# One weight tile per product pass gets its low half from an adding DMA instead of VectorE

## The chip, the cores and the metric

The kernel is one launch on one NeuronCore of a Trainium2 chip. The metric is the device time of that launch in microseconds. A profile of one execution gives the span from the first to the last instruction of the program and every engine's instructions inside it. The engines are TensorE (PE in the profile; its weight loads are PEld), VectorE (DVE), ScalarE (ACT), GpSimd (POOL) and SyncE (SP). DMAs are issued from the instruction queues of SP, ACT and POOL and carried by 16 DMA engines.

## The reference, cut to what matters

The program is one layer of a decoder trunk on 256 tokens of width 2048, all in float32. The change lies in the feed-forward part, which is the last two lines of the layer:

```python
h = rms_norm(x, norm2_gain[l]) * (1 + scale2) + shift2
x = x + gate2 * swiglu(h, w_ffn_in[l], w_ffn_out[l])

def swiglu(h, w_ffn_in, w_ffn_out):
    gate, up = jnp.split(h @ w_ffn_in, 2, axis=-1)
    return (jax.nn.silu(gate) * up) @ w_ffn_out
```

The weights are `w_ffn_in` (2048 x 11264) and `w_ffn_out` (5632 x 2048). Ahead of it come the modulation from `c`, the input projection, three kinds of token mixing and the output projection.

## The kernel before

**Precision by halves.** TensorE is fed in a rounded float32 format (`F32R`). To keep float32 accuracy, every operand is held as a high half (the value rounded to that format) and a low half (value minus high half). A product then takes three matmuls, in `mm3` (L163 to L166): high by high (L164), high of the activations by low of the weights (L165), low of the activations by high of the weights (L166). Activations are the stationary operand, weights the moving one.

**A weight tile.** Weights arrive from HBM in tiles called `raw` of 128 partitions x 2 blocks of 128 rows x 512 columns, 512 KB each, by a DMA on SP's queue. ScalarE makes the high half `whi` by a copy into the rounded format. VectorE makes the low half `wlo` by subtracting the high half from `raw`. `raw`, `whi` and `wlo` each have four buffers that are used in rotation, so a tile's halves can be written once the tile four places earlier has had its last matmul.

**Where the work around the change lies.** The first feed-forward product runs over 11 units of 512 gate columns and 512 up columns. Units 1 to 7 (`FAST`) and the second product go through `fast_products` (L1296), which takes the contraction in pairs of row blocks, in an order that is written out: `PAIRS` for a unit, `OUT_A` and `OUT_B` for the two passes of the second product (columns 0 to 1023 and 1024 to 2047). An entry `(p, 0)` is a plain pair: two weight tiles, one for the columns at `c0` and one for those at `c1`, and 24 matmuls: the 12 of the tile at `c0`, then the 12 of the tile at `c1`. An entry `(p, 1)` is a fast pair: seven products (21 matmuls) on sums of weight blocks, with four tile slots taken in the rotation (`r0`, half of `r1`, and the two sum tiles `ta` and `tb`).

The entries that the change meets are those with `p = 2` that are plain: the fourth entry of `PAIRS` (behind the fast pair 6 and ahead of the fast pair 7), the third entry of `OUT_A` (behind two plain pairs) and the fourth entry of `OUT_B` (behind the fast pair 8).

**What sets the order.** The weights of a pair are requested three pairs ahead (`LOOK = 3`, L35, L1322) under `prio()`, which moves the loads and their splits ahead of other work in each engine's instruction order. Each engine runs its own instructions in the order in which they stand, and waits on semaphores. `load_pair` (L1264) is the function that loads and splits a pair; its inner `split` (L1272) holds the cast (L1276) and the subtraction (L1277), `raw_at` (L1267) the load (L1269). POOL issues some small loads in the first microseconds (L241 to L244), does one cast (L605), and is idle from then on.

Of the kernel before, what the change touches and what calls it, by code (L numbers as in the profile page):

```python
# [10 lines left out]
F32 = mybir.dt.float32  # L11
F32R = mybir.dt.float32r
U8 = mybir.dt.uint8
AF = mybir.ActivationFunctionType
ALU = mybir.AluOpType
AX = mybir.AxisListType

P = 128
# [5 lines left out]
NB = 512  # L24
# [8 lines left out]
RATE_IN, RATE_MID, RATE_FFN = 0.8, 0.6, 0.65  # L33
RATE_OUT = 2.5
LOOK = 3  # L35
DEFER = 4
AHEAD = 4000
WARM = (22, 38, 13)
# [38 lines left out]
def trunk(ctx: ExitStack, tc: tile.TileContext, I, out):  # L77
    nc = tc.nc
# [10 lines left out]
    def nm(base):  # L89
        uid[0] += 1  # L90
        return f"{base}_{uid[0]}"

    def S(tag, shape, dtype=F32):
        return slot.tile(shape, dtype, tag=tag, name=nm(tag))
# [13 lines left out]
    @contextmanager  # L108
    def prio(offset=AHEAD):

        with tc.high_priority(offset=offset):
            start = tc.cur_priority
            yield
            n = tc.cur_priority - start
        tc.cur_priority += n

    state = {"rate": 0.0}
# [4 lines left out]
    def tick(n):  # L122
        state["due"] = state.get("due", 0.0) + n
        while state["due"] >= 1.0:
            state["due"] -= 1.0
            for work in (bg, after):
                if work and next(work[0], "end") == "end":
                    work.pop(0)
# [39 lines left out]
    def block(pss, act, src, k0, k1, c0, base=0, w=None, tiles=range(NT), go_on=False, more=False, seeded=False,  # L168
# [7 lines left out]
        for k in range(k0, k1):  # L176
            if (k - k0) % 2 == 0 and tiles[-1] == NT - 1:
                tick(state["rate"])
            if k - k0 == DEFER and later:
                with tc.issue_after(state["mm"].ins), prio():  # L180
# [895 lines left out]
    for j in range(2):  # L1076
        hi = S(gtag[0][j], [P, 4, T], F32R)
        lo = S(gtag[1][j], [P, 4, T], F32R)
        for t in range(NT):
            o = og[t].rearrange("p h d -> p (h d)")  # L1080
            ps = misc_bank([P, 4, P])
            for i in range(4):
                c = 4 * j + i
                nc.tensor.transpose(ps[:, i, :], o[:, c * P : (c + 1) * P], ident)
            for par in range(2):
                gcol = vec[:, ROW_GG + par : ROW_GG + par + 1]
                src = ps[:, par:4:2, :]
# [176 lines left out]
    def load_pair(src, p, c0, c1, fast, tags):  # L1264


        def raw_at(c):  # L1267
            raw = wp.tile([P, 2, NB], F32, tag="raw", name=nm("raw"))
            nc.sync.dma_start(raw, src[2 * p * P : (2 * p + 2) * P, c : c + NB].rearrange("(k p) c -> p k c", p=P))  # L1269
            return raw  # L1270

        def split(src):  # L1272
            n = src.shape[1]
            hi = wp.tile([P, 2, NB], F32R, tag="whi", name=nm("whi"), bufs=4)
            lo = wp.tile([P, 2, NB], F32R, tag="wlo", name=nm("wlo"), bufs=4)
            nc.scalar.copy(hi[:, :n, :], src)  # L1276
            state["split"] = nc.vector.tensor_tensor(lo[:, :n, :], src, hi[:, :n, :].bitcast(F32), op=ALU.subtract)  # L1277
            return [(hi[:, i, :], lo[:, i, :]) for i in range(n)]

        sub = lambda dst, x, y: nc.vector.tensor_tensor(dst, x, y, op=ALU.subtract)  # L1280
        with prio():
            if not fast:
                return [split(raw_at(c0)), split(raw_at(c1))]
            r0, r1 = raw_at(c0), raw_at(c1)
            b11, b21 = split(r0)
            ta, tb = (S(tag, [P, 2, NB]) for tag in tags)
            sub(ta[:, 0], r1[:, 0], r0[:, 0])
            sub(ta[:, 1], r1[:, 1], r1[:, 0])
            (b22,) = split(r1[:, 1:2])
            sub(tb[:, 0], r1[:, 1], ta[:, 0])  # L1290
            sub(tb[:, 1], r0[:, 1], tb[:, 0])
            t1, t3 = split(ta)
            t2, t4 = split(tb)
            return b11, b21, b22, t1, t3, t2, t4

    def fast_products(src, c0, c1, order, at, sums, own, other, tags, hooks={}, more=False):  # L1296
# [4 lines left out]
        def load(n):  # L1301
            while len(ws) < min(n, len(order)):
                ws.append(load_pair(src, order[len(ws)][0], c0, c1, order[len(ws)][1], tags))

        load(LOOK if hooks else len(order))
        o = [[own([P, NB]) for _ in range(NT)] for _ in range(2)]
# [11 lines left out]
        for n, (p, fast) in enumerate(order):  # L1318
            tick(2 * state["rate"])
            if n in hooks:  # L1320
                hooks[n]()
            load(n + LOOK)  # L1322
            w = ws[n]
# [44 lines left out]
    for i in range(NFF):  # L1368
# [26 lines left out]
        hi = S(ftags[2 * i], [P, 4, T], F32R)  # L1395
        lo = S(ftags[2 * i + 1], [P, 4, T], F32R)
# [61 lines left out]
    n, pss = 3, o[1]  # L1458
# [43 lines left out]
```

## Time and profile before

| | |
|---|---|
| time, median of 3 runs (lowest to highest) | 1597.94 us (1597.09 to 1598.45) |
| the profiled execution's own time | 1597.22 us |
| its span, first to last instruction | 1595.4 us |
| TensorE busy | 1582.0 us, 99% |
| VectorE busy | 1275.5 us, 80% |
| ScalarE busy | 837.6 us, 53% |
| GpSimd busy | 5.3 us |
| bytes moved by DMA | 395.97 MB |

The profiled execution's time is 1.8 us over its span and 0.7 us under the median. The units 1 to 7 run from 918 us to 1220 us of the span, the first pass of the second product (`OUT_A`) from 1353 us, its second pass (`OUT_B`) from 1475 us.

In the rows of the profile, a group of instructions is given by its line in the kernel, the engine, the operation and the names of the tiles it writes and reads, with the count, the busy time and the mean of one in ns. A row of the timeline begins with the start in us from the span's start and the duration in us; in square brackets stands how long the engine was idle before it, and what ended that. The duration of a DMA row on a queue is that of issuing it; "us to landing" is from the start of issue until its last byte has been reported.

### The profile page before, as it was taken

How to read it: one execution, taken by the hardware profiler on the slowest of the kernel's cores; microseconds unless marked ns; L12 is line 12 of the kernel's file. 1: busy time of each engine (PE TensorE's matmuls, PEld its weight loads, DVE VectorE, ACT ScalarE, POOL GpSimd, SP SyncE). 2: the span in 40 equal slices, each digit the busy share in tenths (PEclk: the TensorE clock that was granted, in tenths of full speed). 3: DMA queues.
4: the chain of work that ended last, by engine and by line, in shares of the span. 5: the costliest groups of instructions: out<-in, count | busy, mean ns of one | idle time of the engine just before them, and what ended most of it. 6: DMA issues, size and time to landing. Idle time of an engine off the chain costs nothing.

```text
span 1595.4 us, 20167 instructions
## 1 busy us (share of the span) xinstructions
PE 1582.0 (99%) x7272; PEld 1308.2 (82%) x7272; DVE 1275.5 (80%) x1523; ACT 837.6 (53%) x1184; POOL 5.3 (0%) x14
## 2 busy tenths in 40 slices
PE   8999999999999999999999999999999999999998
PEld 7878888888888888888887888888888888778887
DVE  6889995888878787878756688888887677988884
ACT  5654449775754434444446655555454443554552
POOL 1000000000000000000000000000000000000000
PEclk9999999999999999999999999999999999999999
DMA  9999997667778889989766466556657889667664
GB/s 339 365 326 320 332 302 245 214 189 257 247 258 280 297 301 314 311 289 310 228 192 210 149 196 195 192 184 193 205 183 226 281 302 314 203 196 225 212 204 140
DMA packets 194596, 395.97 MB, mean 248 GB/s; under 512 B 12914, under 2 KB 27928, under 8 KB 194496
## 3 DMA queue, kind: packets, MB, share of 16 engines
q1 hardware_dynamic: 194096, 394.60, 75.0%
q8 instruction: 57, 0.93, 0.2%
q14 instruction: 43, 0.35, 0.1%
q10 hardware_dynamic: 176, 0.07, 0.0%
q0 software_dynamic: 224, 0.01, 0.0%
HBM read 392.53 MB, written 2.10 MB: 247 GB/s over the span
## 4 chain that ended last, share of the span: by engine, by line
PE 85%; DMA 5%; DVE 5%; ACT 3%; issue 2%; SPq 0%; ACTq 0%; DVEq 0%
PE acc L166 21%; PE acc L165 21%; PE acc L164 20%; PE misc L164 6%; PE misc L166 6%; PE misc L165 6%; DVE wlo L159 1%; ACT whi L158 1%; DMA AR<-w_ada 1%; DVE ada L288 1%; DMA raw<-w_br_gla 1%; DMA raw<-w_ffn_out 1%; PE acc L434 1%; DMA raw<-w_in 1%; PE misc L800 1%
## 5 line engine op out<-in xcount | busy, mean ns | idle before, releaser
L158 ACT CAST whi<-raw 128x1024 fp32r<-128x1024 f32 x362 | 368.6, 1022 | 412.2 <-PE acc L166 264.9
L159 DVE TENSOR_TENSOR wlo<-raw,whi 128x1024 fp32r<-128x1024 f32 x362 | 425.6, 1183 | 186.0 <-ACT whi L158 184.4
L164 PE MATMUL acc<-whi,H 128*128 128x512 f32 x1308 | 511.9, 392 | 1.2 <-ACT H L446 0.8
L165 PE MATMUL acc<-wlo,H 128*128 128x512 f32 x1308 | 510.9, 391 | 0.8 <-DVE wlo L159 0.7
L166 PE MATMUL acc<-whi,H 128*128 128x512 f32 x1308 | 509.8, 390 | 0.4 <-DVE H L453 0.4
L166 PEld LDWEIGHTS acc<-whi,H 128*128 128x128 f32 x1308 | 245.3, 188 | 52.9 <-DVE H L453 1.6
L164 PEld LDWEIGHTS acc<-whi,H 128*128 128x128 f32 x1308 | 245.5, 188 | 52.3 <-ACT H L446 1.3
L165 PEld LDWEIGHTS acc<-wlo,H 128*128 128x128 f32 x1308 | 245.7, 188 | 51.3 <-DVE wlo L159 1.7
L1276 ACT CAST whi<-raw 128x1024 fp32r<-128x1024 f32 (+1 forms) x184 | 179.2, 992 | 134.5 <-PE acc L166 68.0
L1277 DVE TENSOR_TENSOR wlo<-raw,whi 128x1024 fp32r<-128x1024 f32 (+1 forms) x184 | 205.2, 1145 | 19.8 <-ACT whi L1276 18.8
L164 PE MATMUL misc<-whi,H 128*128 128x512 f32 x246 | 96.1, 391 | 0.0
L165 PE MATMUL misc<-wlo,H 128*128 128x512 f32 x246 | 95.8, 389 | 0.0
L166 PE MATMUL misc<-whi,H 128*128 128x512 f32 x246 | 95.8, 389 | 0.0
L164 PE MATMUL acc<-whi,A 128*128 128x512 f32 x222 | 87.1, 394 | 0.5 <-ACT whi L1276 0.4
L165 PE MATMUL acc<-wlo,A 128*128 128x512 f32 x222 | 86.7, 390 | 0.8 <-DVE wlo L159 0.8
L166 PE MATMUL acc<-whi,A 128*128 128x512 f32 x216 | 84.3, 390 | 0.0
L288 DVE SCALAR_TENSOR_TENSOR ada<-AR,csil,ada 128x1024 f32<-128x1024 f32 x59 | 74.8, 1278 | 3.6 <-DMA AR<-w_ada 3.6
L165 PEld LDWEIGHTS misc<-wlo,H 128*128 128x128 f32 x246 | 46.2, 188 | 9.7 <-DVE wlo L1277 0.2
L166 PEld LDWEIGHTS misc<-whi,H 128*128 128x128 f32 x246 | 46.2, 188 | 9.5
L164 PEld LDWEIGHTS misc<-whi,H 128*128 128x128 f32 x246 | 46.2, 188 | 9.5
L164 PEld LDWEIGHTS acc<-whi,A 128*128 128x128 f32 x222 | 41.7, 188 | 9.6 <-ACT whi L1276 1.1
L165 PEld LDWEIGHTS acc<-wlo,A 128*128 128x128 f32 x222 | 41.7, 188 | 9.6 <-DVE wlo L159 1.1
(428 smaller groups left out, 1927.6 us busy)
## 6 DMA issues: line engine op xcount, KB each, us to landing
raw<-w_in SPq DMA_DIRECT2D x205, 512.0 KB, 4.8
raw<-w_ffn_in SPq DMA_DIRECT2D x176, 512.0 KB, 4.2
raw<-w_ffn_out SPq DMA_DIRECT2D x88, 512.0 KB, 4.8
AR<-w_ada SPq DMA_DIRECT2D x79, 512.0 KB, 5.1
raw<-w_out SPq DMA_DIRECT2D x32, 512.0 KB, 4.8
KC<-w_ada SPq DMA_DIRECT2D x30, 512.0 KB, 6.2
OS<-w_ada SPq DMA_DIRECT2D x16, 512.0 KB, 6.9
KD<-w_ada SPq DMA_DIRECT2D x16, 512.0 KB, 5.8
```

The lines of the kernel that those rows point to most:

```text
L158: state["cast"] = nc.scalar.copy(hi[:, :n, :], raw[:, :n, :])
L159: state["split"] = nc.vector.tensor_tensor(lo[:, :n, :], raw[:, :n, :], hi[:, :n, :].bitcast(F32), op=ALU.subtract)
L164: nc.tensor.matmul(ps, lh, rh, start=start, stop=False, skip_group_check=seeded)
L165: nc.tensor.matmul(ps, lh, rl, start=False, stop=False, skip_group_check=seeded)
L166: state["mm"] = nc.tensor.matmul(ps, ll, rh, start=False, stop=stop, skip_group_check=seeded)
L288: nc.vector.scalar_tensor_tensor(acc, raw, c, acc, op0=ALU.mult, op1=ALU.add)
L434: state["warm"] = nc.tensor.matmul(ps, ones_r, wide, start=True, stop=True)
L800: nc.tensor.matmul(ps[:n, t * N_GLA + h, :].rearrange("p (s l) -> p s l", l=L), at(f, h, t)[:, :n], odd(at(f, h, t)), start=True, stop=True,)
L1276: nc.scalar.copy(hi[:, :n, :], src)
L1277: state["split"] = nc.vector.tensor_tensor(lo[:, :n, :], src, hi[:, :n, :].bitcast(F32), op=ALU.subtract)
```

## The change

In `split`, a tile for which the weights' address is passed in as `again` gets its low half in two steps: ScalarE writes minus the high half into `wlo`, and a DMA issued from POOL's queue reads the same weights from HBM a second time and adds them to what stands in `wlo`. VectorE's subtraction isn't issued for that tile. It is passed in for the tile at `c1` of every plain pair with `p` in `ADDED`, which is `(2,)`: seven tiles in the units and one in each pass of the second product, nine in all.

```diff
+ADDED = (2,)
...
+        def weights(c):
+            return src[2 * p * P : (2 * p + 2) * P, c : c + NB].rearrange("(k p) c -> p k c", p=P)
+
         def raw_at(c):
             raw = wp.tile([P, 2, NB], F32, tag="raw", name=nm("raw"))
-            nc.sync.dma_start(raw, src[2 * p * P : (2 * p + 2) * P, c : c + NB].rearrange("(k p) c -> p k c", p=P))
+            nc.sync.dma_start(raw, weights(c))
             return raw
 
-        def split(src):
+        def split(src, again=None):
...
             nc.scalar.copy(hi[:, :n, :], src)
-            state["split"] = nc.vector.tensor_tensor(lo[:, :n, :], src, hi[:, :n, :].bitcast(F32), op=ALU.subtract)
+            if again is None:
+                state["split"] = nc.vector.tensor_tensor(lo[:, :n, :], src, hi[:, :n, :].bitcast(F32), op=ALU.subtract)
+            else:
+
+                nc.scalar.activation(lo, hi.bitcast(F32), AF.Copy, scale=-1.0)
+                nc.gpsimd.dma_start(lo, again, accum_op=ALU.add)
             return [(hi[:, i, :], lo[:, i, :]) for i in range(n)]
...
             if not fast:
-                return [split(raw_at(c0)), split(raw_at(c1))]
+                return [split(raw_at(c0)), split(raw_at(c1), weights(c1) if p in ADDED else None)]
```

## The prediction

> **What bounds the kernel now.** I read the page first: busy time, then the chain of work that ended last.
>
> ```profile
> span 1595.4 us, 20167 instructions
> ...
> PE 1582.0 (99%) x7272; PEld 1308.2 (82%) x7272; DVE 1275.5 (80%) x1523; ACT 837.6 (53%) x1184; POOL 5.3 (0%) x14
> ...
> PE 85%; DMA 5%; DVE 5%; ACT 3%; issue 2%; SPq 0%; ACTq 0%; DVEq 0%
> ```
>
> TensorE is busy for all but 13.4 us of the span. So what another engine saves is worth nothing unless TensorE was waiting for it, and any new wait of TensorE is paid in full. Next I asked for the stretches in which the nine tiles lie: units 1 and 2, the beginning of the first output pass, the beginning of the second.
>
> ```profile
> core 0: us, PE busy (x) PEld busy (x) DVE busy (x) ACT busy (x) POOL busy (x), PEclk, DMA share, GB/s
> 918.10:961.20 43.10, 43.10 (x195) 35.75 (x195) 35.93 (x43) 22.36 (x25) 0.00 (x0) 1.00 0.61 196
> ...
> 1352.80:1375.00 22.20, 21.38 (x100) 17.45 (x99) 20.30 (x21) 9.44 (x11) 0.00 (x0) 1.00 0.87 292
> 1475.20:1510.00 34.80, 34.80 (x155) 28.84 (x154) 29.58 (x35) 18.13 (x19) 0.00 (x0) 1.00 0.69 217
> ```
>
> In a unit TensorE is busy for 43.10 of 43.10 us; VectorE, at 35.93 us, is close behind but nobody waits for it. Then I followed one of the tiles on each engine: pair 2 of unit 1, ScalarE, VectorE, TensorE.
>
> ```profile
> 931.53 3.05 ACT L1276 CAST whi<-raw 128x1024 fp32r<-128x1024 f32 x3 [0.30 <-PE misc L166]
> ...
> 933.13 4.09 DVE L1277 TENSOR_TENSOR wlo<-raw,whi 128x1024 fp32r<-128x1024 f32 x4
> ...
> 934.69 0.39 PE L164 MATMUL misc<-whi,H 128*128 128x512 f32 x1
> ...
> 937.41 0.39 PE L164 MATMUL misc<-whi,H 128*128 128x512 f32 x1
> 937.63 0.39 PE L165 MATMUL misc<-wlo,H 128*128 128x512 f32 x1
> ```
>
> The three casts are the tile at c0, the tile at c1 (ours) and the first of fast pair 7. Each takes a third of 3.05 us, so ours ends near 933.55. It can't start much earlier: the first cast was released by TensorE's matmul, that is by a buffer of the rotation. VectorE's four subtractions run one after the other; ours is the second and ends near 935.5. TensorE begins the plain pair at 934.69, needs our high half at 937.41 and our low half at 937.63. So today the low half is about 2.1 us early, and it comes 4.1 us before its use at the very best, since the high half ends there.
>
> **The change part by part.**
>
> *VectorE's subtraction goes, nine times.*
>
> ```profile
> L1276 ACT CAST whi<-raw 128x1024 fp32r<-128x1024 f32 (+1 forms) x184 | 179.2, 992 | 134.5 <-PE acc L166 68.0
> L1277 DVE TENSOR_TENSOR wlo<-raw,whi 128x1024 fp32r<-128x1024 f32 (+1 forms) x184 | 205.2, 1145 | 19.8 <-ACT whi L1276 18.8
> ...
> L165 PE MATMUL acc<-wlo,H 128*128 128x512 f32 x1308 | 510.9, 391 | 0.8 <-DVE wlo L159 0.7
> ```
>
> That frees about 9 x 1.2 = 11 us of VectorE, but TensorE's costliest group of low-half matmuls waits 0.8 us for VectorE in the whole run, and in a unit it waits for nothing. Worth: 0. The `raw` buffer is freed when ScalarE is done (933.55) instead of VectorE (935.5), so SP's next load goes out up to 2 us earlier; TensorE doesn't wait for loads in the units, so 0 again.
>
> *ScalarE's second pass comes in.* It is an activation of 128x1024. No row has that shape; the two rows of 128x512 show an activation and a cast to take the same.
>
> ```profile
> 957.33 0.60 ACT L1387 ACTIVATE scr<-misc 128x512 f32<-128x512 f32 x1 [0.30 <-PE misc L166]
> ...
> 966.85 0.62 ACT L1276 CAST whi<-raw 128x512 fp32r<-128x512 f32 x1 [1.66 <-PE acc L166]
> ```
>
> So I take 1.0 us, as the casts. ScalarE is busy for half of a unit (22.36 of 43.10 us). Queued behind it is the first cast of pair 7, 1.0 us later; its first matmul comes after pair 2, at 934.69 + 24 x 0.227 = 940.1, over 4 us after that cast would end. Covered. The negated half is there at 933.55 + 1.0 = 934.55. From here to 937.63 are **3.1 us**, in which the DMA has to be issued and land.
>
> *The adding DMA.* The trace has no DMA of 512 KB from POOL and none that adds. These rows lie nearest.
>
> ```profile
> raw<-w_ffn_in SPq DMA_DIRECT2D x176, 512.0 KB, 4.2
> raw<-w_ffn_out SPq DMA_DIRECT2D x88, 512.0 KB, 4.8
> ...
> H<-c SPq DMA_DIRECT2D x1, 8.0 KB, 1.5
> H<-sb_q_gain POOLq DMA_DIRECT2D x1, 0.5 KB, 3.8
> ...
> H<-c POOLq DMA_DIRECT2D x1, 8.0 KB, 5.4
> ```
>
> ```profile
> L1269 SPq DMA_DIRECT2D raw<-w_ffn_in x112: 367/368/368, 901.6 to 1203.7; - x112
> ...
> DMA to landing us min/median/max: 3.6/4.4/7.0
> ```
>
> ```profile
> 1.43 0.63 POOL L241 DMA_DIRECT2D H<-sb_q_gain  x1
> ...
> 934.38 3.84 SPq L1269 DMA_DIRECT2D raw<-w_ffn_in  x4
> ```
>
> A load of the same size from SP lands in 4.2 us, 3.6 at the least: already over 3.1. Of these 4.2 us, 1.5 are there for almost no bytes (8 KB from SP) and 2.7 belong to the 512 KB. From POOL almost no bytes (0.5 KB) take 3.8 us, 0.63 of it issue. So plain bytes from POOL make 3.8 + 2.7 = 6.5 us. Adding means that the tile is read as well as written; if that doubles the bytes' share it makes 3.8 + 2 x 2.7 = 9.2 us. The four loads that SP issues from 934.38 on run on the same DMA engines at the same time, so the lower end is not the likely one. I take the middle, **7.9 us**, an estimate from these rows. Lower bound 4.2 (no penalty for POOL or for adding), upper bound some 12 (9.2 and another 2.7 for the loads beside it). A cost below nothing is excluded: the low half can't be ready before its DMA has landed.
>
> Issuing from POOL holds up nobody: POOL is idle in all these stretches (0.00 busy), and SP's and ACT's queues don't carry it. It moves 9 x 0.5 MB more, 4.7 of 396 MB; the DMA engines are 0.61 busy in the units.
>
> *The new wait.* TensorE's first low-half matmul of the tile waits for the landing, and everything behind it on TensorE with it: 7.9 - 3.1 = **4.8 us** per unit. Nothing gives it back later, for ScalarE and VectorE are paced by TensorE (their casts wait for its buffers). Seven units: 7 x 4.8 = 33.6 us.
>
> For the two output passes the same count from their own rows.
>
> ```profile
> 1359.66 1.06 ACT L1276 CAST whi<-raw 128x1024 fp32r<-128x1024 f32 x1 [1.98 <-DMA raw<-w_ffn_out]
> ...
> 1367.63 0.39 PE L165 MATMUL acc<-wlo,A 128*128 128x512 f32 x1
> ```
>
> ```profile
> 1487.88 3.05 ACT L1276 CAST whi<-raw 128x1024 fp32r<-128x1024 f32 x3 [0.31 <-PE misc L166]
> ...
> 1493.98 0.39 PE L165 MATMUL misc<-wlo,A 128*128 128x512 f32 x1
> ```
>
> In the first pass two plain pairs stand ahead of pair 2. The high half ends at 1360.7, minus it at 1361.7, the use is at 1367.63: 5.9 us of room, a stall of 2.0. In the second pass our cast ends near 1489.9, minus it at 1490.9, the use is at 1493.98: 3.1 us of room, a stall of 4.8.
>
> **Sum**: 33.6 + 2.0 + 4.8 = 40.4 us on the profiled execution's 1597.2 us, which lies 0.7 us under the median of the runs: 1637.6, and with that offset 1638.
>
> *TensorE's clock after a stall.* The two warm-up rows give the price of a cold clock, and the last stretch shows how long TensorE may idle.
>
> ```profile
> 2.58 6.85 PE L434 MATMUL acc<-H,ones_r 128*128 128x512 f32 x22
> ...
> 10.47 9.11 PE L434 MATMUL acc<-H,ones_r 128*128 128x512 f32 x38
> ```
>
> ```profile
> 1590.00:1595.40 5.40, 1.33 (x12) 1.12 (x10) 2.19 (x6) 0.00 (x0) 0.00 (x0) 1.00 0.14 49
> ```
>
> After the idle start 22 matmuls took 6.85 us, where at the later pace (9.11 / 38) they take 5.27: a cold start costs 1.6 us. In the last stretch TensorE works for 1.33 us and then idles for 4.1, and the granted clock is still 1.00. A stall of 4.8 us is just beyond what this row covers, so I leave the cold start out of the sum and carry it as a rival.
>
> **The rivals.**
>
> 1. *Each stall also cools TensorE.* If 4.8 us without matmuls drop the clock, the eight long stalls cost 1.6 us more each: 8 x 1.6 = 13, time 1651. Against it speaks the 4.1 us at clock 1.00; for it, that the drop must lie somewhere beyond. The Trainium skill says in "TensorE: Matmul & The Clock Gate", section "Part 1: The HAM clock gate", that the clock halves after an idle window of about 3.4 us and that the window runs freely; by it most of these stalls would be hit, while the 4.1 us above show that not every one must be.
>
> 2. *The DMA is short.* POOL's 3.8 us stand at the start of the program, beside a burst of loads; in the units the fixed part may be less and adding may cost nothing. With 4.4 us to landing the eight stalls are 1.3 each, the ninth 0: 1608.
>
> 3. *The DMA is long.* At 12 us: 8 x 8.9 + 6.1 = 77, and surely cold after each, 14 more: 1689. For it: the 5.4 us that POOL's last small load took beside other loads.
>
> 4. *Hidden.* From 3.1 us downwards the low half is in time in all nine places, and the time is 1598. That needs a DMA faster than the fastest SP load of this size (3.6). The Trainium skill's "DMA: Bandwidth & Descriptors", section "Anatomy of one DMA", would nearly allow it: about 2.0 us fixed plus the bytes at 436 GB/s, an estimate of 3.2 us for 512 KB; the 3.8 us for 0.5 KB contradict the fixed part.
>
> 5. *Faster.* With the DMA in time, VectorE's 11 us could be worth something in the first output pass, the one stretch where TensorE idles (22.20 - 21.38 = 0.8 us). If all of that went, 1597, which is still no measurable gain; a gain of over 0.2% (3.2 us) would need a wait on VectorE that no row shows.
>
> **How the numbers follow.** The forecast (6.5 to 9.2 us to landing, no cooling) spans 8 x 3.4 + 0.6 = 28 to 8 x 6.1 + 3.3 = 52 us, 1626 to 1650: chance 0.55. Rival 1: 0.20. Rival 2: 0.11. Rival 3: 0.08. Rival 4: 0.04. Rival 5: 0.02. The range reaches down to 5 us to landing (8 x 1.9 = 15, 1613) and a little on, 1610, and up to 10 us with the cooling (8 x 6.9 + 4.1 + 13 = 72), 1670. A measurement of this kernel can tell about 0.2% from no change. Faster 0.02, within it 0.04, slower 0.94.
>
> **What would show it.** In the changed kernel's profile: nine DMAs of 512 KB from POOL to `wlo`, at 6.5 to 9 us to landing; nine activations of about 1.0 us that write `wlo`; VectorE some 11 us less busy; TensorE's L165 group with a new idle time of about 40 us ended by that DMA, in nine pieces, the one in the first output pass the smallest; a unit of 47.9 instead of 43.1 us. Matmuls of double length behind each piece would show rival 1. I am wrong if the DMA lands in under 4 us, if minus the high half is not written right after our cast (behind the next cast each stall grows by 1.0), or if the stalls are given back within the unit.

## The result and the profile after

The changed kernel takes 1663.27 us (median of 4 runs, 1660.41 to 1665.92) where the kernel before takes 1598.05: a ratio of 1.041, 95% interval 1.039 to 1.042. It is slower, as forecast, and inside the range of 1610 to 1670, but 25 us above the forecast of 1638. The profiled execution took 1664.83 us, with a span of 1663.0, which is 67.6 us longer than before.

These lines are from the page of the changed kernel (lines 164 to 166 of the kernel before are 165 to 167 now): span and busy times, the chain, two groups of instructions, the DMAs.

```profile
span 1663.0 us, 20196 instructions
...
PE 1603.9 (96%) x7272; PEld 1320.8 (79%) x7272; DVE 1266.7 (76%) x1514; ACT 845.8 (51%) x1193; POOL 16.3 (1%) x23
...
q0 software_dynamic: 2672, 4.73, 1.7%
...
PE 75%; DMA 10%; DVE 7%; ACT 5%; issue 3%; SPq 0%; ACTq 0%; DVEq 0%; POOLq 0%
...
L1282 DVE TENSOR_TENSOR wlo<-raw,whi 128x1024 fp32r<-128x1024 f32 (+1 forms) x175 | 195.6, 1141 | 28.2 <-ACT whi L1280 26.8
...
L166 PE MATMUL misc<-wlo,H 128*128 128x512 f32 x246 | 100.3, 408 | 16.9 <-DMA wlo<-w_ffn_in 16.9
```

The change did what it says: nine subtractions fewer on VectorE (175 instead of 184), which is 8.8 us less busy. TensorE has a new wait, and also a new number: the same 7272 matmuls take 1603.9 us of busy time instead of 1582.0. So TensorE waits *and* works more slowly. Unit 1 on three engines, from the timeline:

```profile
933.45 2.00 ACT L1280 CAST whi<-raw 128x1024 fp32r<-128x1024 f32 x2 [0.30 <-PE misc L167]
935.48 1.06 ACT L1285 ACTIVATE wlo<-whi 128x1024 fp32r<-128x1024 f32 x1
...
936.84 1.28 POOL L1286 DMA_DIRECT2D wlo<-w_ffn_in  x1 [690.33 <-PE misc L167]
...
945.26 0.80 PE L166 MATMUL misc<-wlo,H 128*128 128x512 f32 x1 [5.10 <-DMA wlo<-w_ffn_in]
945.85 0.63 PE L167 MATMUL misc<-whi,H 128*128 128x512 f32 x1
946.28 0.63 PE L165 MATMUL misc<-whi,H 128*128 128x512 f32 x1
```

Minus the high half is ready at 936.54, POOL begins to issue 0.3 us later, and TensorE, which ran out of work at 940.16, goes on at 945.26. From there a matmul begins every 0.43 us, not every 0.227. Stretches of the same trace show the same (the columns are length, busy time of PE, PEld, DVE, ACT and POOL with counts, granted clock, DMA share, GB/s); the first row holds as many matmuls as a unit has:

```profile
918.10:968.30 50.20, 45.10 (x196) 36.94 (x195) 34.45 (x40) 22.63 (x26) 1.28 (x1) 0.93 0.57 178
...
942.30:949.13 6.83, 3.87 (x9) 3.10 (x10) 0.00 (x0) 0.00 (x0) 0.00 (x0) 0.50 0.52 174
949.13:960.00 10.87, 10.87 (x49) 8.96 (x49) 9.02 (x10) 6.84 (x8) 0.00 (x0) 1.00 0.47 153
```

The unit is 50.2 us long instead of 43.1: 5.1 us without work and 2.0 us of slower work, at a granted clock of 0.50 until 949.13. The trace's clock record has such a stretch at half clock for each of the nine tiles, 6.83 us long for seven of them and 3.41 us for two. The group of the adding DMA (L1286) says who waited for it in all, and the list of DMA issues how long it took to land:

```profile
  PE misc L166: 23.2, 5
...
  PE acc L166: 20.0, 4
```

```profile
wlo<-w_ffn_in POOLq DMA_DIRECT2D x7, 512.0 KB, 7.8
...
wlo<-w_ffn_out POOLq DMA_DIRECT2D x2, 512.0 KB, 9.9
```

23.2 + 20.0 = 43.2 us of gaps, nine of them, 3.6 to 6.3 us each. With the 1603.9 - 1582.0 = 21.9 us by which the same matmuls took longer, about 2.4 us for each gap, that makes 65.1 of the 67.6 us.

### The profile page after: what moved, and what is told of

It reads as the page before. It is cut to its first block, busy times and chain, and to the rows that moved or that the text cites. A ratio compares the mean times of both kernels' runs of the same rounds, so it can differ in the third digit from the quotient of the medians.

```text
span 1663.0 us, 20196 instructions
## 1 busy us (share of the span) xinstructions
PE 1603.9 (96%) x7272; PEld 1320.8 (79%) x7272; DVE 1266.7 (76%) x1514; ACT 845.8 (51%) x1193; POOL 16.3 (1%) x23
## 3 DMA queue, kind: packets, MB, share of 16 engines
q0 software_dynamic: 2672, 4.73, 1.7%
## 4 chain that ended last, share of the span: by engine, by line
PE 75%; DMA 10%; DVE 7%; ACT 5%; issue 3%; SPq 0%; ACTq 0%; DVEq 0%; POOLq 0%
PE acc L166 18%; PE acc L167 18%; PE acc L165 18%; PE misc L166 6%; PE misc L167 5%; PE misc L165 5%; DMA wlo<-w_ffn_in 3%; ACT whi L159 2%; DVE wlo L160 2%; DMA AR<-w_ada 2%; DMA wlo<-w_ffn_out 1%; DMA raw<-w_ffn_in 1%; DVE ada L289 1%; DMA raw<-w_br_gla 1%; DMA raw<-w_ffn_out 1%
## 5 line engine op out<-in xcount | busy, mean ns | idle before, releaser
L1282 DVE TENSOR_TENSOR wlo<-raw,whi 128x1024 fp32r<-128x1024 f32 (+1 forms) x175 | 195.6, 1141 | 28.2 <-ACT whi L1280 26.8
L166 PE MATMUL misc<-wlo,H 128*128 128x512 f32 x246 | 100.3, 408 | 16.9 <-DMA wlo<-w_ffn_in 16.9
L167 PE MATMUL misc<-whi,H 128*128 128x512 f32 x246 | 99.4, 404 | 0.0
L165 PE MATMUL misc<-whi,H 128*128 128x512 f32 x246 | 97.6, 400 | 0.3 <-DVE misc L1320 0.3
L1282 DVE TENSOR_TENSOR wlo<-KD,whi 128x1024 fp32r<-128x1024 f32 x14 | 17.1, 1225 | 60.2 <-ACT whi L1280 60.0
L167 PEld LDWEIGHTS misc<-whi,H 128*128 128x128 f32 x246 | 48.7, 198 | 10.4
L165 PEld LDWEIGHTS misc<-whi,H 128*128 128x128 f32 x246 | 47.5, 193 | 10.8 <-issue 0.7
```

The costliest lines, as they stand in the source:

```text
L165: nc.tensor.matmul(ps, lh, rh, start=start, stop=False, skip_group_check=seeded)
L166: nc.tensor.matmul(ps, lh, rl, start=False, stop=False, skip_group_check=seeded)
L167: state["mm"] = nc.tensor.matmul(ps, ll, rh, start=False, stop=stop, skip_group_check=seeded)
```

## The experiments

The theory: the time is the wait of TensorE for the adding DMA plus a slow clock behind each wait. Its rivals: ScalarE's second pass costs by itself; the second read of the weights or POOL's DMA slows other work; the time beyond the gaps is not the clock.

### ScalarE's pass without the DMA

```diff
                 nc.scalar.activation(lo, hi.bitcast(F32), AF.Copy, scale=-1.0)
-                nc.gpsimd.dma_start(lo, again, accum_op=ALU.add)
+                state["split"] = nc.vector.tensor_tensor(lo, lo.bitcast(F32), src, op=ALU.add)
```

> The nine tiles keep ScalarE's pass that writes minus the high half, but VectorE adds the weights from raw to it; no DMA adds. If the time went into the wait for the adding DMA and the cold clock behind it: about 1598, no TensorE gap over 1 us in the units, since minus the high half is there near 934.6, the addition ends by 936.7 and the low half is used at 937.6. If ScalarE's added pass costs by itself: nine times 1.0 us, about 1607.

Measured: 1599.37 us, ratio 1.0005 (0.9996 to 1.0014). ScalarE's pass costs nothing that can be measured. Units 1 and 2 are full:

```profile
918.10:961.20 43.10, 43.10 (x195) 35.76 (x195) 34.90 (x42) 22.75 (x25) 0.00 (x0) 1.00 0.61 195
961.20:1004.30 43.10, 43.10 (x195) 35.74 (x195) 36.21 (x44) 23.22 (x26) 0.00 (x0) 1.00 0.61 195
```

### The same DMA, one pair earlier

```diff
...
+            hi, lo = S("AR0", [P, 2, NB], F32R), S("AR1", [P, 2, NB], F32R)
+            nc.scalar.copy(hi, raw)
+            nc.scalar.activation(lo, hi.bitcast(F32), AF.Copy, scale=-1.0)
+            nc.gpsimd.dma_start(lo, again, accum_op=ALU.add)
...
+                if nxt[0] in ADDED and not nxt[1] and tags[0] == "OD":
+                    early[nxt[0]] = load_added(src, nxt[0], c1)
```

> In the seven units alone, the adding DMA stays, with the same bytes from the same queue, but the tile has high and low buffers of its own and its load, cast, negation and DMA stand one pair earlier, so the low half lands some 8 us before its use. The two output passes use VectorE as before. If only the wait (with the cold clock behind it) costs: 1598 within 3 us, no gap of 1 us, the granted clock 1.00 throughout. If the second read of the weights or POOL's DMA slows other loads or engines: most of the 50 us of the units stay, 1630 or more. If VectorE's saved 1.2 us per unit is worth something: under 1597.

Measured: 1600.22 us, ratio 1.0012 (1.0004 to 1.0021). The seven DMAs are there, as long as in the changed kernel (7.7 us to landing). With buffers of its own the tile need not wait for the rotation: in unit 1 POOL issues at 919.15 us, 17.7 us earlier than in the changed kernel. Units 1 and 2 are as long and as full as before the change:

```profile
AR<-w_ffn_in POOLq DMA_DIRECT2D x7, 512.0 KB, 7.7
```

```profile
918.10:961.20 43.10, 43.10 (x196) 35.78 (x195) 34.86 (x42) 23.09 (x26) 1.28 (x1) 1.00 0.70 207
961.20:1004.30 43.10, 43.10 (x196) 35.77 (x195) 34.94 (x42) 22.63 (x26) 1.21 (x1) 1.00 0.69 207
```

So the second read and POOL's DMA by themselves cost the seven units at most some 2 of the 50 us that they lost; what costs is where the DMA stands. VectorE's saved 1.2 us per unit is worth nothing either. Of the remaining 2 us (0.12%), most lies in one unit, where TensorE waits 0.71 us at 1150 us and 0.20 us at 1152 us for VectorE's subtractions; why VectorE is late there stays open.

### TensorE kept busy during the wait

```diff
...
+                    if c == 1 and p in ADDED and zero is not None:
+                        for _ in range(20):
+                            with tc.issue_after(state["mm"].ins):
+                                nc.tensor.matmul(o[1][0], zero, w[1][0][0], start=False, stop=False, skip_group_check=True)
```

> The changed kernel, with 20 matmuls of a zero tile (adding nothing, 20 x 0.227 = 4.5 us) put on TensorE's queue in each of the seven units ahead of the matmul that waits. If the part of the loss beyond the gaps is the cold clock: the units stay at full clock and shorten from 50.2 to about 48, the time falls from 1663 to about 1648. If that part is contention or a late refill of other buffers: no fall, 1663 or a little above.

Measured: 1648.43 us, ratio 1.032 (1.030 to 1.033). The 20 matmuls stand where the gap was (L1358 in this kernel), and the stretch around them has the full clock:

```profile
940.82 4.70 PE L1358 MATMUL misc<-whi,AR 128*128 128x512 f32 x20
945.36 0.39 PE L165 MATMUL misc<-whi,H 128*128 128x512 f32 x1
```

```profile
938.00:950.00 12.00, 12.00 (x55) 9.94 (x54) 4.24 (x6) 4.24 (x7) 1.28 (x1) 1.00 0.73 218
```

The filling takes about as long as the gaps did (20 x 0.227 = 4.5 us), and the seven units have the full clock throughout; yet the kernel is 1663.27 - 1648.43 = 14.8 us faster, 2.1 us a unit. That is the price of the slow clock, or a little less than it, for TensorE still idles 1.8 us in these units, 1.64 of them in the third, where the DMA came later than the filling ended. The forecast left this price out of its sum.

### The same DMAs where there is more room

```diff
-ADDED = (2,)
+ADDED = (5,)
```

> ADDED = (5,) in place of (2,): the same nine DMAs, but in the units and in the first output pass the tile stands behind two plain pairs, where the rotation lets its cast start 36 matmuls before its use (8.2 us less 0.3, 1.05 and 1.0 of waiting and ScalarE: 5.8 us of room instead of 3.1). If the wait is landing less room: gaps of about 2.5 us in eight places and one of 6, and if a gap of 2.5 us doesn't cool TensorE, about 1598 + 20 + 6 + 2 = 1626; if it does, up to 1642. If each DMA costs a fixed amount wherever it stands: 1663.

Measured: 1617.01 us, ratio 1.011 (1.010 to 1.013). The cost goes with the room. It is even less than expected; the DMA is shorter there, 6.5 us to landing in the units instead of 7.8, seven times 1.3 us. In the units the gaps are at most 1.7 us. In the output passes they are 1.6 and 5.7 us, and only the last was followed by a slow clock. The DMAs of this trace (KB each, us to landing):

```profile
wlo<-w_ffn_in POOLq DMA_DIRECT2D x7, 512.0 KB, 6.5
wlo<-w_ffn_out POOLq DMA_DIRECT2D x2, 512.0 KB, 8.7
```

Who waited for these DMAs (us, times): 11.7 us in all, where the changed kernel has 43.2.

```profile
  PE misc L166: 7.7, 4
...
  PE acc L166: 4.0, 3
```

### What the landing is made of

The next three change the DMA alone: no addition, half the bytes, a thirty-second of the bytes in as many rows.

```diff
-                nc.gpsimd.dma_start(lo, again, accum_op=ALU.add)
+                nc.gpsimd.dma_start(lo, again)
```

> The changed kernel with POOL's DMA writing the weights over the low half instead of adding them, so the low half holds the weights themselves and the product is another; place, queue, bytes and waits are the same. If the addition costs the DMA time (the tile read as well as written): landing falls from 7.8 us in the units to 5.5 to 6.5, the time to about 1640. If adding is free beside the transfer: 7.8 us and 1663 as before.

```diff
-                nc.gpsimd.dma_start(lo, again, accum_op=ALU.add)
+                nc.gpsimd.dma_start(lo[:, 0], again[:, 0], accum_op=ALU.add)
+                state["split"] = nc.vector.tensor_tensor(lo[:, 1], lo[:, 1].bitcast(F32), src[:, 1], op=ALU.add)
```

> The DMA adds only the first of the tile's two blocks (256 KB, 128 rows of 2 KB); VectorE adds the other from raw. If the landing is a fixed part of about 3.8 us and a part that goes by bytes: about 5.8 us in the units instead of 7.8, gaps of 2.5 instead of 4.6 us and hardly a cold clock, about 1625. If the landing is mostly fixed: 7 us or more and over 1645.

```diff
-                nc.gpsimd.dma_start(lo, again, accum_op=ALU.add)
+                nc.gpsimd.dma_start(lo[:, :, :16], again[:, :, :16], accum_op=ALU.add)
+                state["split"] = nc.vector.tensor_tensor(lo[:, :, 16:], lo[:, :, 16:].bitcast(F32), src[:, :, 16:], op=ALU.add)
```

> The DMA adds only 16 of the 512 columns of each block (256 rows of 64 bytes, 16 KB); VectorE adds the rest from raw. If the fixed part is the 3.8 us that POOL's small loads take: landing near 4.3 us with 1.2 of it issue, gaps of about 1.2 us, no cold clock, about 1610. If the number of rows, not the bytes, makes the time: 7 us or more and over 1645.

Measured, with the landing in the units, in us, from the list of DMA issues of each trace:

| POOL's DMA | time | ratio (95% interval) | us to landing |
|---|---|---|---|
| adds 512 KB (the change) | 1663.27 us | 1.041 (1.039 to 1.042) | 7.8 |
| writes 512 KB | 1633.94 us | 1.023 (1.018 to 1.027) | 5.4 |
| adds 256 KB | 1649.15 us | 1.032 (1.024 to 1.041) | 6.7 |
| adds 16 KB in 256 rows | 1633.51 us | 1.022 (1.018 to 1.027) | 5.4 |

These are the rows of the list, first of the version that writes, then of the one with half the bytes, then of the one with 16 KB:

```profile
wlo<-w_ffn_in POOLq DMA_DIRECT2D x7, 512.0 KB, 5.4
```

```profile
wlo<-w_ffn_in POOLq DMA_DIRECT2D x7, 256.0 KB, 6.7
```

```profile
wlo<-w_ffn_in POOLq DMA_DIRECT2D x7, 16.0 KB, 5.4
```

The addition costs 2.4 us at this place. It shows in the DMA queue's own line too: in the version that writes, the 2672 packets take 0.9% of 16 engines' span of 1632.0 us, some 90 ns each; in the changed kernel 1.7% of 1663.0 us, some 170 ns each. POOL's issue is longer as well, by 0.5 us; below are its minimum, median and maximum in ns, first of the version that writes, then of the changed kernel.

```profile
q0 software_dynamic: 2672, 4.73, 0.9%
```

```profile
L1286 POOL DMA_DIRECT2D wlo<-w_ffn_in x7: 713/713/754, 935.5 to 1212.5; - x7
```

```profile
L1286 POOL DMA_DIRECT2D wlo<-w_ffn_in x7: 1194/1197/1279, 936.8 to 1238.5; - x7
```

The expectations on the two small versions missed. Nearly no bytes, 16 KB, still land only after 5.4 us, not 4.3, and the time falls to 1634, not 1610: the fixed part of an adding DMA of 256 rows is 5.4 us here, and all of its 512 KB add only 2.4 to that. How much of the 5.4 us is owed to the loads that SP issues beside it, no version shows.

### Is it POOL's queue?

Two versions read the weights a second time from ScalarE's queue, plainly, into a tile of their own (units only), from which VectorE subtracts. In the first, the read waits for nothing:

```diff
-                nc.gpsimd.dma_start(lo, again, accum_op=ALU.add)
+                if tags[0] == "OD":
+                    src = S("AR0", [P, 2, NB])
+                    nc.scalar.dma_start(src, again)
+                state["split"] = nc.vector.tensor_tensor(lo, src, hi.bitcast(F32), op=ALU.subtract)
```

> In the seven units the second read of the weights is issued from ScalarE's queue, at the same place (behind the high half's cast), into a tile of its own, and VectorE subtracts from that tile; in the output passes VectorE works as before. If POOL's issue is what makes the adding DMA longer than a load from SP: landing at 4.2 to 4.8 us, as SP's loads; the low half is ready some 6.2 us behind the cast, 2 us late in each unit, about 1613. If any load of this size put at this place takes 7.8 us, because of the loads beside it: 9 us behind the cast, 5 us late, over 1640.

Measured: 1599.69 us, ratio 1.0007 (0.9995 to 1.0018), no new gap. The experiment did not ask what it was meant to ask. In its timeline VectorE subtracts from the tile at 935.70 and the read is issued behind that, at 936.95: it is the read for the next unit. Since nothing tied it to ScalarE's pass, it had been placed a whole unit early.

```profile
936.95 0.39 ACTq L1288 DMA_DIRECT2D AR<-w_ffn_in  x1
...
935.70 1.22 DVE L1289 TENSOR_TENSOR wlo<-AR,whi 128x1024 fp32r<-128x1024 f32 x1
```

In the second, ScalarE's negation writes into the tile that the read overwrites, so that the read has to stand behind it:

```diff
...
+                    src = S("AR0", [P, 2, NB])
+                    nc.scalar.activation(src, hi.bitcast(F32), AF.Copy, scale=-1.0)
+                    nc.scalar.dma_start(src, again)
...
```

> As the run before with the read from ScalarE's queue, but now ScalarE first writes minus the high half into the tile that the read overwrites, so that the read has to wait for that pass, at the place where POOL's DMA waits in the changed kernel; VectorE then subtracts from that tile. Seven units only. If 512 KB read plainly from that queue land in 4.2 to 5.0 us at this place: the low half is ready some 6 us behind ScalarE's pass, against 8.6 in the changed kernel, gaps of about 2.3 us instead of 4.6, some of them with a cold clock: 1614 to 1628. If the loads beside it make any DMA at this place long: landing at 7 us or more and over 1640.

Measured: 1636.96 us, ratio 1.024 (1.021 to 1.027), above the 1614 to 1628 expected. The one landing that the trace gives is 5.4 us (the row of the list stands first below), and in unit 1 the read is issued at 935.69 and VectorE begins with it at 941.43, 5.7 us later.

```profile
AR<-w_ffn_in ACTq DMA_DIRECT2D x7, 512.0 KB, 5.4
```

```profile
935.69 0.40 ACTq L1288 DMA_DIRECT2D AR<-w_ffn_in  x1
...
941.43 1.23 DVE L1289 TENSOR_TENSOR wlo<-AR,whi 128x1024 fp32r<-128x1024 f32 x1 [5.46 <-DMA AR<-w_ffn_in]
```

So a plain read at this place takes as long from ScalarE's queue (5.4) as from POOL's (5.4); the issuing queue is not what makes the DMA long. By the Trainium skill's "DMA: Bandwidth & Descriptors", section "Issuing engines are not separate DMA queues", DMAs run on the same 16 DMA engines whichever engine started them; these two landings agree. What goes on beside the read may count: in the first of these two versions the reads of the units from the second on, issued from the same queue (in unit 1 at 936.95, 1.3 us later), landed in 3.8 to 5.1 us, 4.3 in the median. The time came out higher than expected because six of the seven gaps, though only 2.0 to 4.0 us long, were followed by a slow clock.

## Why the prediction was right or wrong

*"Worth: 0" for VectorE, and "covered" for ScalarE's pass.* Right. The version with ScalarE's pass alone is at 1.0005, the one with the DMA out of the way at 1.0012.

*The room of 3.1 us.* Nearly right. POOL needed 0.3 us from the end of ScalarE's pass to its issue, which the prediction hadn't counted, and TensorE did two matmuls more ahead of the wait than before, which gave 0.45 us back.

*The landing of 7.9 us.* Right as a total in the units (7.8), wrong in its parts, so partly by luck: it was the middle between a free addition (6.5) and a doubled one (9.2). The prediction had 3.8 fixed and the rest bytes, doubled for the addition. Measured are 5.4 for a plain read at this place from either queue, and 2.4 for the addition. The 4.2 us of SP's loads was reached at this place from neither queue.

*A stall of 4.8 us in seven units.* Right: the seven gaps are 5.10, 4.50, 3.60, 5.40, 4.01, 5.05 and 4.16 us, 4.55 in the mean.

*2.0 and 4.8 us in the output passes.* Too small: 5.05 and 6.33. The landing was taken from the units; in these passes it is 9.9.

```profile
1426.56 0.79 PE L166 MATMUL acc<-wlo,A 128*128 128x512 f32 x1 [5.05 <-DMA wlo<-w_ffn_out]
...
1560.59 0.80 PE L166 MATMUL misc<-wlo,A 128*128 128x512 f32 x1 [6.33 <-DMA wlo<-w_ffn_out]
```

The gaps together are 43.2 us where the prediction had 40.4.

*"I leave the cold start out of the sum."* This is the step that failed. Rival 1, given a chance of 0.20, is what happened, for every one of the nine gaps, and it was priced at 1.6 us where the filled gaps show 2.1 or a little more and TensorE's busy time about 2.4. The 1.6 us came from one cold start at the beginning of the program; in the changed kernel the half clock lasted 6.83 us seven times, though TensorE was still idle for part of it. Matching the two traces matmul by matmul gives the 27.2 us that the sum of 40.4 lacks of the 67.6: some 21 us for the slow clock, 2.8 us more of gaps, 1.9 us that are there before the units begin, ahead of any tile that the change meets, and 1.4 us of other idle time in the output passes. The result is inside the range only because its upper end was worked out with the cooling: the forecast without it spans 1626 to 1650.

One inference of rival 1 doesn't follow either. If a whole window of 3.4 us has to be idle, a stall of 4.8 us at a random place holds such a window in about 0.4 of all cases, an estimate ((4.8 - 3.4) / 3.4), not in most.

The row that misled was the end of the kernel before, 4.1 us of idle at clock 1.00. Cut differently, it shows something else:

```profile
1589.58:1592.99 3.41, 1.75 (x15) 1.54 (x13) 2.27 (x6) 0.00 (x0) 0.00 (x0) 1.00 0.11 38
1592.99:1595.40 2.41, 0.00 (x0) 0.00 (x0) 0.00 (x0) 0.00 (x0) 0.00 (x0) 1.00 0.16 54
```

The trace's clock record says that the clock was halved at 1596.40 us, just behind the span. The idle did cool TensorE; the program had ended before it showed.

## What to carry to other kernels

Work that is moved to a DMA brings the DMA's whole latency into the chain of its consumer, here 9.8 us from the end of the cast (935.45 to 945.26 in unit 1) in place of VectorE's 1.9; it is free only where the consumer is further away than that, and the same DMA one pair earlier was, to within 2 us. Where TensorE is the bound, a new gap can cost more than its length: add some 2 us for the slow clock behind it. In these traces that held for each gap from 3.6 us on, for some of those between 1.97 and 3.5 us, and for none that was shorter. And relief for an engine that nobody waits for is worth nothing, whatever its busy share.

## What was not expected

**The clock is decided window by window.** In the clock records of all these traces, the stretches at half clock, but for the last, which the end of the record cuts off, are 3.41 or 6.83 us long, and those at full clock between them are multiples of 3.41 us too (44.37 is 13 of them). So there is a fixed grid of 3.41 us. Take the windows of the grid that hold part of a gap over 1 us or of the time behind the last matmul, in the eleven traces of this case, and reckon how much of each TensorE was idle: up to 0.52 of a window, the clock stayed full at its end in every case; above 0.56 it was halved in every case; between, both occurred. Idle time is not the whole rule, though: one window without such a gap was followed by half clock too, that from 29.44 to 32.85 us in the version with the 20 matmuls, where TensorE was busy for 2.60 us, in part with matmuls of 1 and of 128 columns; the kernel before is busy there for 2.61 us and kept its clock. The version with the plain DMA has one of each: gaps of 1.99 and 2.17 us, the shorter of which cooled TensorE because it lay within one window. Below, each first row is the window with the idle, each second row the one behind it.

```profile
1215.81:1219.22 3.41, 1.42 (x7) 1.20 (x7) 1.23 (x1) 0.41 (x1) 0.00 (x0) 1.00 1.09 369
1219.22:1222.63 3.41, 3.41 (x10) 2.64 (x9) 0.22 (x1) 1.30 (x2) 0.00 (x0) 0.50 0.14 52
1075.86:1079.27 3.41, 1.56 (x7) 0.94 (x6) 1.96 (x3) 1.05 (x1) 0.00 (x0) 1.00 1.12 382
1079.27:1082.69 3.42, 3.11 (x14) 2.56 (x15) 0.00 (x0) 0.46 (x1) 0.00 (x0) 1.00 0.59 219
```

TensorE busy for 1.42 of 3.41 us: halved; for 1.56: not. The Trainium skill's "TensorE: Matmul & The Clock Gate", section "Part 1: The HAM clock gate", has the free-running window of 3413 ns and a return to half clock after at least one idle window. The window agrees with the records; that it must be idle throughout, if that is meant, does not. The border lies near 0.55 of it, so a gap of 2.0 us cost the clock, while one of 3.5 us (in the version that adds 256 KB, at 1539 us), split about evenly between two windows, did not.

**The fixed part of an adding DMA.** 16 KB added in 256 rows landed no sooner (5.4 us) than 512 KB written plainly (5.4 us).
